# Hybrid attention block on one core: in the first seven attention units a group's fill is written ahead of the products of the group behind it

## The chip, the cores and the metric

The kernel runs on 1 core of a Trainium2 chip. A core has a matrix engine (TensorE, in the profile PE for matmuls and PEld for weight loads), VectorE (DVE), ScalarE (ACT), GpSimd (POOL) and SyncE (SP, which here only starts transfers). The metric is the device time of one execution in microseconds; less is better.

## The reference

A decoder block on x (1024 rows of 1024), all in float32. It normalises x, projects it, and runs two attention branches on the projections: "fox", 8 heads of width 64 with a forgetting bias, and "diff", 4 heads with two query and key pairs each, whose softmaxes are subtracted. Cut to what matters:

```python
h = rms_norm(x, g_pre)
qa, ka, va, fa, za, qb, kb, vb, zb, gates = split(h @ w_in)
ya = merge(fox(qa, ka, va, log_sigmoid(fa + b))) * silu(za)     # softmax(q k^T / 8 + c_t - c_s) v
qd, kd = rope(qb), rope(kb)
yb = merge((softmax(q1 k1^T) - lam * softmax(q2 k2^T)) vb)      # per diff head
yb = rms_norm(yb, g_subln) * (1 - lam_init) * silu(zb)
merged = sigmoid(g_a) * (ya @ w_branch[0]) + sigmoid(g_b) * (yb @ w_branch[1])
out = x + rms_norm(merged @ w_out, g_post)
```

## The kernel before

**Number format.** Every float32 operand of a large matmul is split in a high part (rounded) and a low part (the rest), and a product is three matmuls (high by high, high by low, low by high) or two. So each matrix needs a cast (ACT or POOL) and a subtraction (mostly DVE) before PE can use it.

**Stages.** First x is normalised and transposed to hT and the values are projected (L214, up to about 107 us). Then come eight attention units: units 0 to 3 are the diff heads, units 4 to 7 two fox heads each. Then the gates (L830, x_g), the branch matrices (L990) and the output matrix (L830, x_o) follow.

**One attention unit.** Queries are taken in groups of 256 rows. A diff unit has four groups, g = 0 to 3, in this order; a fox unit has eight, g = 3, 3, 2, 2, 1, 1, 0, 0 (two heads each). A group with index g sees 256(g+1) keys. It has two parts in the text:

- *Rows* (`s_row`, L492 to L501, and `row`): the logits Sd or Sf by two matmuls, a DVE instruction that scales them, adds the bias and finds the extreme (L495), the exponential on ACT, and the scaling of the result. In diff units POOL and ACT scale the two softmaxes (L592, L594) and POOL adds them (L595). The result lies in tiles Pd or Pf, six of them in all.
- *Products* (`products`, `av`): P is transposed in blocks on PE (ptd or ptf, L522; 4g + 3 transposes a group), cast on ACT (L525), the rest subtracted on DVE (L526), and multiplied with V (ypd or ypf, L546). The result is taken out (ACT L602, or ACT L632 and DVE L633) and stored in y_d.

**The fill.** Beside its groups each unit has a list of other work, `fill`: the four chunks that project the next unit's keys and queries (pk and pq, L334, each 24 matmuls of 128x512 on a bank of pool `pj`, which has two), in most units two chunks of a z projection (pz; four in unit 7), and in units 3 to 6 the sums of squares of an earlier diff head (`sum_squares`, ssq, L448 and L449, and a small transfer task). A chunk of a diff unit's key or query is rotated afterwards: ACT copies it (L362), four transfers swap its parts (L366), DVE multiplies (L368), POOL multiplies the swapped part (L369) and DVE adds (L370). Then every key or query chunk is split (L378, L379) and copied to its tiles (L381, L382); a z chunk is copied and stored. The first chunk of each matrix loads its weights (`load_w`, L314 to L324).

**The order in the text.** Each unit's loop goes over its groups. After a group's rows come the products of the group before it (`pend`, across the border of two units too), and then as many fill tasks as bring the done share of the list up to the done share of the unit's weights, 4g + 3 a group. In unit 7 the share is tripled and the loop ends differently (a tail that is written by hand, with gate pieces put after given matmuls).

**The order on the chip.** The kernel is built with `schedule_with_timeline_sim=True`: the framework plans, from the text, in which order each engine gets its instructions, so that matmuls of rows, products and fill come mixed on PE. Tiles, banks and semaphores are set by it as well.

Of the kernel before, what the change touches and what calls it, by code (L numbers as in the profile page):

```python
# [50 lines left out]
def tile_hybrid_block(  # L51
# [288 lines left out]
    with ExitStack() as st:  # L340
# [75 lines left out]
        def z_tasks(t):  # L416
            return spill_tasks(f"z{t}", (ZA + t * P) if t < 4 else (ZB + (t - 4) * P), z_d[t])
# [20 lines left out]
        def sum_squares(t, c):  # L438

            sl = slice(c * CH, (c + 1) * CH)  # L440
            sq = stg.tile([P, CH], F32, tag="raw", name=f"sq{t}_{c}", bufs=4)
            nc.sync.dma_start(sq, y_d[t][:, sl])
            nc.scalar.activation(sq, sq, AF.Square)
            hi, lo = (stg.tile([P, CH], F32R, tag="sw", name=f"sq{part}{t}_{c}") for part in range(2))
            nc.scalar.copy(hi, sq)
            nc.gpsimd.tensor_tensor(lo, sq, hi, op=ALU.subtract)
            ps = pj.tile([P, CH], F32, tag="pj", name=f"ssq{t}_{c}")[0:32]
            nc.tensor.matmul(ps, lhsT=onesr, rhs=hi, start=True, stop=False)  # L448
            nc.tensor.matmul(ps, lhsT=onesr, rhs=lo, start=False, stop=True)  # L449
            nc.scalar.copy(sq[0:1], ps[0:1])  # L450
            nc.sync.dma_start(ss_d[t:t + 1, sl], sq[0:1])

        def subln_scales(t):
            rs = sub_rs[:, t]
            nc.sync.dma_start(rs, ss_d[t].rearrange("(p j) -> p j", j=8))
            rstd_of(rs, rs, P, SUB_EPS)
            nc.sync.dma_start(rs_d[t].rearrange("(p j) -> p j", j=8), rs)
# [96 lines left out]
        def products(trans, prod, g):  # L554
            for jj in range(g + 1 + SKEW):
                if jj <= g:
                    trans(jj)
                if jj >= SKEW:
                    prod(jj - SKEW)
# [91 lines left out]
        def forget_sums():  # L651

            fgf = fg.rearrange("p a b -> p (a b)")
            fs = pp.tile([P, 4, 64], F32, tag="P", name="fs")
            fn, fe, fu, fc = (fs[:, n, :] for n in range(4))
            nc.vector.tensor_scalar(fn, fgf, -1.0, None, op0=ALU.mult)
            nc.vector.tensor_tensor(fn, fn, fgf, op=ALU.min)
            nc.scalar.activation(fe, fn, AF.Exp)
            nc.vector.tensor_scalar(fu, fe, 1.0, None, op0=ALU.add)
            nc.vector.tensor_scalar(fc, fu, -1.0, None, op0=ALU.add)  # L660
            nc.vector.tensor_tensor(fc, fe, fc, op=ALU.subtract)
            nc.scalar.activation(fn, fu, AF.Ln)
            nc.vector.reciprocal(fu, fu)
            nc.vector.tensor_tensor(fc, fc, fu, op=ALU.mult)
            nc.vector.tensor_tensor(fn, fn, fc, op=ALU.add)
            nc.vector.tensor_scalar(fe, fgf, 0.0, None, op0=ALU.min)
            nc.vector.tensor_tensor(fe, fe, fn, op=ALU.subtract)
            lf = pp.tile([8, S], F32, tag="P", name="lf")
            cum = pp.tile([8, S], F32, tag="P", name="cum")
            ones8 = pp.tile([8, S], F32, tag="P", name="ones8")  # L670
            nc.gpsimd.memset(ones8, 1.0)
            for half in range(2):
                tp = tps.tile([P, CH], F32, tag="tp", name=f"ft{half}")
                for q in range(4):
                        b = half * 4 + q
                        nc.tensor.transpose(tp[0:8, q * P:(q + 1) * P], fe[:, b * 8:(b + 1) * 8], ident)
                nc.scalar.copy(lf[:, half * CH:(half + 1) * CH], tp[0:8, :])
            nc.vector.tensor_tensor_scan(cum, ones8, lf, initial=0.0, op0=ALU.mult, op1=ALU.add)
            nc.vector.tensor_scalar(cum, cum, -8.0, None, op0=ALU.mult)
            nc.sync.dma_start(cum_d, cum)  # L680
# [7 lines left out]
        for u in range(8):  # L688
            load, load_v, groups = nxt or unit_attn(u, T)
            nxt = None  # L690
            if u == 0:
                vload.append(load_v)
            if u == 1:
                forget_sums()
            load()
            fill = []
            if u + 1 < 8:
                T, tasks = unit_proj(u + 1)
                fill += tasks
            for t in ZFILL[u]:  # L700
                fill += z_tasks(t)
            for t in SFILL[u]:
                fill += [lambda t=t, c=c: sum_squares(t, c) for c in range(2)]
                fill.append(lambda t=t: subln_scales(t))
            late = [fill.pop(), gate[0]] if u == 7 else []
            total = sum(s[0] for s in groups)
            done, nf = 0, 0
            for n, (wgt, rws, prd) in enumerate(groups):
                if n == len(groups) // 2 and u < 7:
                    nxt = unit_attn(u + 1, T)  # L710
                    vload.append(nxt[1])
                for r in rws:
                    r()
                mark = lasts[0]
                if pend and (u < 7 or n <= TAIL):
                    products(*pend())
                if u == 7 and n >= TAIL:
                    tail.append(prd)
                pend = prd
                done += wgt  # L720
                while nf < len(fill) and nf < len(fill) * done * (3 if u == 7 else 1) / total:
                    fill[nf]()
                    nf += 1
                if u == 7:
                    for f, a, b in LATE[n]:
                        with tc.issue_after(mark):
                            late[f](range(a, b))
                    if n == GFILL:
                        break
# [503 lines left out]
```

## Time and profile before

| | |
|---|---|
| median of 3 runs | 900.85 us (899.52 to 901.63) |
| the profiled execution | 899.54 us, of which 897.8 us from first to last instruction |
| HBM traffic | 139 GB/s over the span |
| PE, mean of one 128x512 matmul of a fill chunk (pq, high part) | 395 ns as recorded; matmuls overlap |
| one transposing matmul (ptd) | 272 ns as recorded, the median |
| cast (phd, ACT) and subtraction (pld, DVE) after it | 567 and 680 ns, medians |
| POOL's sum of two softmaxes (L595) | 454 to 2899 ns, median 1438 |

The profile is of one execution. Busy time of an engine is the time in which at least one of its instructions runs; waits are idle time of an engine just before an instruction, put down to whatever ended last. In a timeline row the first number is the start in us from the first instruction, the second the length of the merged instructions, x the count, and a bracket gives the idle time before it and what ended it.

### The profile page before, as it was taken

What the parts mean: (1) busy time and instruction counts of PE and PEld (TensorE: products, weight loads), DVE (VectorE), ACT (ScalarE), POOL (GpSimd) and SP (SyncE); (2) the same over time, 40 slices, a digit from 0 to 9 for tenths busy, and PEclk for the clock granted to TensorE, in tenths of its full rate; (3) what the DMA queues carried; (4) which work ended last, traced back from release to release, by engine and by line L of the source; (5) the groups of instructions that cost most, each with busy time, mean ns of one, the idle gap of its engine ahead of it and who ended that gap; (6) DMA issues with size and microseconds to landing.
All of it is one profiled execution on the core that took longest, in us unless ns stands there. A gap on an engine that the chain in (4) does not pass through costs nothing.

```text
span 897.8 us, 13825 instructions
## 1 busy us (share of the span) xinstructions
PE 881.9 (98%) x4612; PEld 746.7 (83%) x4612; DVE 580.4 (65%) x1124; ACT 429.0 (48%) x864; POOL 408.9 (46%) x401
## 2 busy tenths in 40 slices
PE   8999999999999999999999999999999999999997
PEld 6999987788888888888888888888888888888885
DVE  6666555767666744456647556626776897648896
ACT  7423224665756654365545646624453362314352
POOL 2234224645646535254344435426534323483963
PEclk9999999999999999999999999999999999999999
DMA  8576656756657763635636430297766599210495
GB/s 306 188 254 245 215 164 158 179 137 170 155 137 184 183 177 77 187 94 133 188 94 155 141 106 30 88 411 240 235 202 213 168 359 312 78 41 1 123 197 172
DMA packets 138186, 154.81 MB, mean 172 GB/s; under 512 B 12145, under 2 KB 98161, under 8 KB 137090
## 3 DMA queue, kind: packets, MB, share of 16 engines
q1 hardware_dynamic: 133744, 151.55, 56.1%
q0 software_dynamic: 4224, 2.10, 2.1%
q8 instruction: 37, 0.61, 0.3%
q14 instruction: 35, 0.29, 0.1%
q10 hardware_dynamic: 146, 0.27, 0.1%
HBM read 86.17 MB, written 38.34 MB: 139 GB/s over the span
## 4 chain that ended last, share of the span: by engine, by line
PE 87%; DMA 3%; DVE 3%; SPq 2%; ACT 2%; POOL 2%; issue 1%; POOLq 0%; DVEq 0%; ACTq 0%
PE x_g L830 15%; PE pv L214 10%; PE pb L990 10%; PE pz L334 9%; PE x_o L830 8%; PE pk L334 7%; PE pq L334 7%; PE ypf L546 3%; PE ptf L522 3%; PE ypd L546 2%; PE Sf L492 2%; PE Sf L493 2%; PE ptd L522 1%; PE Sd L492 1%; PE Sd L493 1%
## 5 line engine op out<-in xcount | busy, mean ns | idle before, releaser
L214 PE MATMUL pv<-wvhi,hT 128*128 128x264 f32 (+2 forms) x384 | 88.6, 325 | 0.0
L334 PE MATMUL pq<-hT,hi_q 128*128 128x512 f32 x256 | 82.1, 395 | 0.0
L334 PE MATMUL pz<-hT,hi_z 128*128 128x512 f32 x256 | 81.6, 394 | 0.4 <-DVE rotq L368 0.3
L334 PE MATMUL pk<-hT,hi_k 128*128 128x512 f32 x256 | 81.7, 393 | 0.0
L990 PE MATMUL pb<-yT,hi_br 128*128 128x512 f32 x256 | 79.0, 389 | 0.0
L830 PE MATMUL x_g<-T,a_g 128*128 128x512 f32 x336 | 78.0, 391 | 0.0
L830 PE MATMUL x_o<-wo_op,a_o 128*128 128x512 f32 x324 | 74.8, 392 | 0.0
L830 PEld LDWEIGHTS x_g<-T,a_g 128*128 128x128 f32 x336 | 63.1, 188 | 13.8
L830 PEld LDWEIGHTS x_o<-wo_op,a_o 128*128 128x128 f32 x324 | 60.7, 188 | 13.9 <-DVE a_o L767 0.5
L214 PEld LDWEIGHTS pv<-wvhi,hT 128*128 128x128 f32 x384 | 64.8, 192 | 5.7
L526 DVE TENSOR_TENSOR plf<-ptf,phf 128x512 fp32r<-128x512 f32 (+1 forms) x80 | 50.1, 635 | 25.1 <-ACT phf L525 24.4
L501 ACT ACTIVATE Pd<-Pd,mxd 128x128 f32<-128x128 f32 (+7 forms) x64 | 49.8, 779 | 33.4 <-DVE mxd L495 33.3
L618 POOL TENSOR_TENSOR cb<-cb,trim 128x128 f32<-128x128 f32 x64 | 29.3, 462 | 74.6 <-DVE mxf L495 51.6
L214 PE MATMUL pv<-wvlo,hT 128*128 128x256 f32 (+2 forms) x192 | 61.7, 326 | 0.0
L501 ACT ACTIVATE Pf<-Pf,mxf 128x1024 f32<-128x1024 f32 (+3 forms) x64 | 49.8, 779 | 24.5 <-DVE mxf L495 22.4
L830 PE MATMUL x_g<-hT,a_g 128*128 128x512 f32 x252 | 59.1, 392 | 0.0
L623 POOL TENSOR_SCALAR Pf<-Pf,lf 128x1024 f32<-128x1024 f32 (+3 forms) x64 | 47.9, 753 | 20.9 <-DVE lf L622 17.6
L525 ACT CAST phf<-ptf 128x512 fp32r<-128x512 f32 (+1 forms) x80 | 42.6, 543 | 30.7 <-PE ptf L522 26.4
L990 PEld LDWEIGHTS pb<-yT,hi_br 128*128 128x128 f32 x256 | 48.0, 188 | 10.4 <-issue 0.4
L830 PEld LDWEIGHTS x_g<-hT,a_g 128*128 128x128 f32 x252 | 47.3, 188 | 10.4
L334 PEld LDWEIGHTS pz<-hT,hi_z 128*128 128x128 f32 x256 | 47.3, 188 | 9.5 <-DVE rotq L368 0.6
L334 PEld LDWEIGHTS pq<-hT,hi_q 128*128 128x128 f32 x256 | 47.2, 188 | 8.9
(277 smaller groups left out, 2289.2 us busy)
## 6 DMA issues: line engine op xcount, KB each, us to landing
t_d<-t SPq DMA_DIRECT2D x16, 512.0 KB, 4.0
T<-t_d SPq DMA_DIRECT2D x8, 1024.0 KB, 11.0
raw<-in_w_in_dram SPq DMA_DIRECT2D x14, 512.0 KB, 5.5
vb_d<-vbs SPq DMA_DIRECT2D x8, 512.0 KB
va_d<-vas SPq DMA_DIRECT2D x8, 512.0 KB, 3.8
raw_k<-in_w_in_dram SPq DMA_DIRECT2D x8, 512.0 KB, 4.4
raw_q<-in_w_in_dram SPq DMA_DIRECT2D x8, 512.0 KB, 4.7
V<-vb_d SPq DMA_DIRECT2D x4, 1024.0 KB, 6.2
```

The source lines that it names most:

```text
L214: nc.tensor.matmul(ps[n], lhsT=hT[hp][k // 4][i // 4][:, k % 4, hs], rhs=wt[k][:, a:b], start=first, stop=(k == KT - 1 and hp == 1))
L334: mm = nc.tensor.matmul(ps, lhsT=a[:, k, :], rhs=hT[h][k // 4][c][:, k % 4, :], start=(k == 0 and a is hi and h == 0), stop=(k == KT - 1 a ...
L492: nc.tensor.matmul(ps, lhsT=A[:, qs], rhs=B[:, a:b], start=True, stop=False)
L501: nc.scalar.activation(pr[:, 0:n], pr[:, 0:n], AF.Exp, bias=mx[:, len(pcs) - 1:len(pcs)], scale=-1.0, accum_out=le)
L522: lasts[0] = nc.tensor.transpose(pt[:, o * P:(o + 1) * P], rows[2 * g + r][:, j * P:(j + 1) * P], ident).ins
L525: nc.scalar.copy(ph[:, 0:n], pt[:, 0:n])
L526: nc.vector.tensor_tensor(pl[:, 0:n], pt[:, 0:n], ph[:, 0:n], op=ALU.subtract)
L546: lasts[0] = nc.tensor.matmul(o, lhsT=a, rhs=b[:, src], start=(j == 0 and n == 0), stop=(odd == 1 and jj == g and n == len(prods) - 1)).ins
L618: nc.gpsimd.tensor_tensor(diag, diag, trim, op=ALU.add)
L623: held[0] = nc.gpsimd.tensor_scalar(p1[:, 0:n], p1[:, 0:n], l1, 1.0, op0=ALU.mult, op1=ALU.mult).ins
L830: nc.tensor.matmul(x[m], lhsT=a[:, ai, k, :], rhs=right[m][bi][k], start=(k == 0 and n == 0), stop=(k == 3 and n == 2))
L990: nc.tensor.matmul(ps, lhsT=a[:, kk, :], rhs=yT[g][h][:, k % 2, sl], start=(k == 0 and a is hi and h == 0), stop=(k == 3 and a is lo))
```

## The change

In units 0 to 6 a group's fill share moves from behind the products of the group before it to ahead of them. The share is as large as before; unit 7 keeps its order. No instruction is added or removed, no tile changes its size or its number of buffers.

```diff
                 for r in rws:
                     r()
                 mark = lasts[0]
+                done += wgt
+
+                def more(nf):
+                    while nf < len(fill) and nf < len(fill) * done * (3 if u == 7 else 1) / total:
+                        fill[nf]()
+                        nf += 1
+                    return nf
+
+                if u < 7:
+                    nf = more(nf)
                 if pend and (u < 7 or n <= TAIL):
                     products(*pend())
                 if u == 7 and n >= TAIL:
                     tail.append(prd)
                 pend = prd
-                done += wgt
-                while nf < len(fill) and nf < len(fill) * done * (3 if u == 7 else 1) / total:
-                    fill[nf]()
-                    nf += 1
+                nf = more(nf)
                 if u == 7:
                     for f, a, b in LATE[n]:
                         with tc.issue_after(mark):
```

So for group n, with R for rows, P for products and F for a fill share, the text read R(n), P(n-1), F(n), R(n+1), P(n), F(n+1); it now reads R(n), F(n), P(n-1), R(n+1), F(n+1), P(n).

## The prediction

> **What bounds the kernel now.** First the page, for the engine that has no room; then the busy time by stage; then the waits of that engine; last its timeline, for the order of its work.
>
> ```profile
> span 897.8 us, 13825 instructions
> PE 881.9 (98%) x4612; PEld 746.7 (83%) x4612; DVE 580.4 (65%) x1124; ACT 429.0 (48%) x864; POOL 408.9 (46%) x401
> PEclk9999999999999999999999999999999999999999
> PE 87%; DMA 3%; DVE 3%; SPq 2%; ACT 2%; POOL 2%; issue 1%; POOLq 0%; DVEq 0%; ACTq 0%
> ```
>
> TensorE (PE) is busy 881.9 of 897.8 us, at full granted clock in every slice, and holds 87% of the chain that ended last. VectorE (DVE), the next compute engine, is at 65%. So only idle time of PE can be won. Where it lies, from the busy time of each engine in three stretches (the attention units run from about 107 to 592 us; I put the borders at 154 and 530 us for reasons given below):
>
> ```profile
> core 0: us, PE busy (x) PEld busy (x) DVE busy (x) ACT busy (x) POOL busy (x), PEclk, DMA share, GB/s
> 107.00:154.00 47.00, 45.75 (x210) 37.36 (x209) 25.70 (x52) 16.24 (x37) 13.81 (x14) 1.00 0.57 158
> 154.00:530.00 376.00, 372.52 (x2082) 319.40 (x2080) 227.40 (x580) 209.53 (x443) 185.06 (x201) 1.00 0.57 148
> 530.00:592.00 62.00, 60.68 (x369) 52.39 (x369) 38.27 (x111) 39.05 (x85) 29.65 (x41) 1.00 0.31 112
> ```
>
> In the long middle stretch PE idles 376.00 - 372.52 = 3.48 us. The waits of PE in it, with who ended them (total, times, longest):
>
> ```profile
> PE ptd L522 <- POOL Pd L595: 0.9, 1, 0.9
> PE Sd L492 <- DVE mxd L495: 0.6, 2, 0.4
> PE ssq L448 <- ACT sq L445: 0.5, 1, 0.5
> PE pz L334 <- DVE rotq L368: 0.3, 1, 0.3
> PE ypf L546 <- DVE ys L633: 0.3, 1, 0.3
> PE ypf L546 <- DVE plf L526: 0.2, 1, 0.2
> PE ptf L522 <- DVE plf L526: 0.2, 1, 0.2
> ```
>
> They sum to 3.0 us. The products wait 0.9 + 0.3 + 0.2 + 0.2 = 1.6 us of it (transposes ptd, ptf and matmuls ypf), the fill 0.5 + 0.3 = 0.8 us (ssq, pz), the logits 0.6 us (Sd). No wait is as long as 1 us. A wait costs more than its idle time. A 128x512 matmul is recorded with 0.39 us but followed by the next after 0.23 (24 of them in 5.49 us, below), so the first 0.16 us of a delay don't show as idle; and the pair that starts after the wait at 171.11 (below) takes 0.72 where others take 0.62. That makes 0.26 us more at each of the eight waits, an estimate of 2.1 us in all.
>
> **What the planned order already does.** The text of the kernel isn't the order on PE: a matmul chain written in one piece is broken up on the chip by whatever else was ready in the framework's planning. What stands earlier in the text goes first when both are ready. So it matters where the fill already runs ahead of the products. Unit 1, PE's timeline:
>
> ```profile
> 187.55 0.62 PE L334 MATMUL pq<-hT,hi_q 128*128 128x512 f32 x2
> ...
> 194.35 0.39 PE L334 MATMUL pq<-hT,lo_q 128*128 128x512 f32 x1
> 194.58 0.40 PE L334 MATMUL pk<-hT,hi_k 128*128 128x512 f32 x1
> 194.82 1.03 PE L522 MATMUL ptd<-ident,Pd 128*128 128x128 f32 x8
> ```
>
> The pq chunk is the fill share of unit 1's second group; the eight transposes at 194.82 are the first of unit 0's last group. In the text those products stand ahead of this whole chunk, and of the one before it, but their rows were not ready, so two chunks of fill went first. The swap changes nothing there. The other kind of place, unit 0:
>
> ```profile
> 153.69 0.61 PE L334 MATMUL pq<-hT,hi_q 128*128 128x512 f32 x2
> 154.15 0.27 PE L522 MATMUL ptd<-ident,Pd 128*128 128x128 f32 x1
> 154.17 0.48 PE L334 MATMUL pq<-hT,lo_q 128*128 128x512 f32 x1
> ...
> 158.20 0.40 PE L334 MATMUL pq<-hT,lo_q 128*128 128x512 f32 x1
> 159.50 0.76 PE L522 MATMUL ptd<-ident,Pd 128*128 128x128 f32 x5 [0.90 <-POOL Pd L595]
> ```
>
> Here a transpose of the second group breaks into the fill share of the third: products were ready first, and the swap turns the two round. Following chunks and products by name through the whole timeline, I count 30 fill shares with products pending behind them in units 0 to 6; in 17 of them the products start before the share's last matmul. 154.15 is the first of the 17; none lies in unit 6, whose products start after the projections of their share. In unit 7, from 530 us on, the text stays as it was. So the first and last stretch should keep their idle time, but for what is handed on from the middle.
>
> **The change part by part.** It adds and removes no instruction: PE's 2082 matmuls of the middle stretch stay, each of the same shape. What moves is a share, one to three chunks. A chunk costs PE this, in the chain of work that ended last (start, us, what):
>
> ```profile
> 107.55 5.49 PE pk L334 x24
> ```
>
> So 5.49 us a chunk, and products that were ready may be put off by 5.5 to 16 us at the 17 places, the fill brought forward by the length of the products that it overtakes. Work that only changes places on a busy engine costs nothing: 0 us, as long as something ready stands next on PE. Changing between transposes and other matmuls could have had a price; the row that follows the eight transposes of 194.82 bounds it:
>
> ```profile
> 195.61 0.47 PE L334 MATMUL pk<-hT,hi_k 128*128 128x512 f32 x1
> ```
>
> It takes 0.47 against 0.39 us in the rows above, so under 0.1 us a change, and as many changes go as come. I take 0.
>
> What each wait of PE becomes. (a) 159.50, 0.9 us: the fill of that share was done at 158.60 and the next chunk (pz) began at 161.12 in the same timeline, so nothing was ready. With the fill first the same work is done by then in another order, and the wait stays: 0. (b) The logits' 0.6 us: they stand ahead of both in the text, as before: 0. (c) The products' other 0.7 us (ys, plf, three waits, with 3 x 0.26 us 1.5): these follow a transpose or an evacuation that the plan took as just in time. Products that go later stand behind a reserve: between 0 and -1.5, I take the middle, -0.7. (d) ssq 0.5: its chunk now stands ahead of the products, which must cover the same chain of load, square and cast; between -0.5 and +0.5, I take 0. (e) pz 0.3: it waits for a bank that the rotation of an earlier chunk must leave. This kind grows, because fill that is placed as soon as the plan thinks it ready has no reserve: between 0 and the second rival's price; I take one more such wait, 0.28 + 0.26 = +0.5.
>
> The share's other engines move too. Its transfers on SP's queue (weights, half swaps, stacked copies) go ahead of the products' stores of y_d, which nobody reads for a whole unit or more:
>
> ```profile
> 160.57 0.54 SPq L603 DMA_DIRECT2D y_d<-ys  x1
> 161.16 0.46 SPq L382 DMA_DIRECT2D TB<-loq  x1
> 161.71 2.46 SPq L366 DMA_DIRECT2D swk<-rawk  x4
> ```
>
> The loads of X that the next group needs stand behind both in the text: 0. On POOL the products have nothing. On DVE they do; its longest kind of wait in a rotation, over the whole run, and one rotation with the PE row that waited for it:
>
> ```profile
> DVE rotq L370 <- POOL swq L369: 15.1, 7, 5.2
> ```
>
> ```profile
> 170.36 0.69 DVE L368 TENSOR_TENSOR rotq<-pq,cosT 128x512 f32<-128x512 f32 x1 [0.34 <-ACT rawq L362]
> ...
> 171.11 0.72 PE L334 MATMUL pz<-hT,hi_z 128*128 128x512 f32 x2 [0.28 <-DVE rotq L368]
> ```
>
> The sum of a rotation (rotq L370) waits for POOL, 15.1 us in 7 times, and what DVE has next waits with it. Products' subtractions that used to go ahead of it may now queue behind it, and PE's products behind them. Unseen in this trace; between 0 and the 2.2 us of one such wait. I take 0, since rows nearest to it (the two 0.2 us waits for plf) say that PE feels little of DVE.
>
> Sum of (a) to (e) and the queues: 0 + 0 - 0.7 + 0 + 0.5 + 0 = -0.2 us. The profiled execution took 899.54 us, 1.7 us more than its span; the median of the runs is 900.85 (899.52 to 901.63). -0.2 us from the median gives **900.6 us**. What a measurement can tell from no change here is about 0.2%, 1.8 us.
>
> [...]
>
> **The rivals.** *Faster: the reserve pays.* Products placed behind a share of fill no longer meet rows or casts that are late on the chip, also at (a), because the plan itself comes out otherwise. For it: 1.6 of the 3.0 us are waits of products. Against it: half of them has nothing else to run. Price: the 3.48 us of idle time and the 2.1 us hidden beside it are all there is; the products' part, 1.6 us and four times 0.26, gives -2.6: 898.2 us. *Slower: the fill becomes what is late.* At 170.36 the rotation left its bank 11.8 us after its chunk's last matmul (158.6), more than the 5.49 us that a following chunk fills. Written first, a share takes its second chunk up as soon as the plan sees the bank free, and a chip that is a little later than the plan stops PE at its head, with the products behind it. The place is the start of a chunk in the 17 turned shares; its price is 0.54 us each, 0.28 of 171.11 and 0.26 beside it. With every second of them hit, 9 x 0.54 = 4.9 us, 905.7 us; it decides from 4 on (2.2 us). Against it: units 3 to 6 fill mostly with chunks that need no rotation. *It does nothing:* the plan turns little round even at the 17 places; 900.85 us, inside the forecast's case.
>
> **How the numbers follow.** Forecast, within 0.2%: 0.38, since 13 of 30 shares keep their order and in the others work only trades places on a full engine. Faster: 0.32. Slower: 0.30; the ceiling of a gain is low, but nothing bounds a loss as tightly. Range: down to all idle time of the middle stretch gone with half of what hides beside it (900.85 - 3.5 - 1.1 = 896.2), up to the second rival's 905.7 and the 0.8 us by which the slowest run shown lies over the median: 906.5.
>
> **What would show it.** The two traces should agree up to about 154 us, where the pq chunk should now run through without the transpose. PE's matmul count should stay; PE's idle time in the middle stretch should stay between 2 and 5 us, with fewer waits of ptf and ypf and more of pk, pq or pz for rotation or POOL. I am wrong if PE idles over 6 us there (the fill is late, or DVE holds the products), under 1.5 us (the reserve was worth more), or if the last units, whose text hardly changes, differ much: then the order planned at the end hangs on what comes before.

## The result, and the profile after

The changed kernel takes 911.34 us (median of 6 runs, 908.4 to 919.27), the kernel before 900.5 us (6 runs, 899.03 to 901.63). The ratio is 1.0129, with a 95% interval from 1.0088 to 1.0169. The forecast was no change, 900.6 us, and its range ended at 906.5 us; the time lies outside it. The profiled execution took 909.24 us.

The page of the changed kernel, first the busy times, then the engines' shares of the chain that ended last:

```profile
span 907.5 us, 13827 instructions
PE 884.3 (97%) x4612; PEld 748.2 (82%) x4612; DVE 575.7 (63%) x1124; ACT 428.9 (47%) x864; POOL 409.1 (45%) x401
PE 73%; DMA 8%; POOL 5%; DVE 5%; issue 3%; ACT 3%; SPq 2%; POOLq 0%; DVEq 0%; ACTq 0%
```

The count of matmuls is the same. PE was busy only 2.4 us longer, the span grew by 9.7 us, and PE's share of the last chain fell from 87% to 73%: PE waits for others now. Where, from the busy time of each engine by stretch (columns as before: stretch, its length, busy time and instructions of PE, PEld, DVE, ACT, POOL, granted clock, DMA):

```profile
154.00:200.00 46.00, 42.60 (x218) 35.31 (x217) 31.30 (x73) 26.97 (x52) 25.91 (x20) 0.96 0.59 146
200.00:262.00 62.00, 61.78 (x343) 52.96 (x343) 38.29 (x102) 36.99 (x83) 33.17 (x29) 1.00 0.56 139
262.00:330.00 68.00, 67.05 (x362) 56.93 (x360) 39.48 (x102) 38.09 (x81) 36.01 (x32) 1.00 0.71 184
330.00:430.00 100.00, 97.60 (x549) 84.31 (x550) 52.64 (x135) 49.07 (x102) 42.74 (x52) 1.00 0.50 131
430.00:530.00 100.00, 96.64 (x559) 83.56 (x558) 57.61 (x160) 53.40 (x117) 43.81 (x62) 1.00 0.49 133
530.00:592.00 62.00, 60.69 (x383) 52.66 (x382) 41.99 (x123) 39.88 (x91) 28.50 (x45) 1.00 0.22 68
```

Length less PE's busy time gives its idle time. From 154 to 530 us it is 3.40 + 0.22 + 0.95 + 2.40 + 3.36 = 10.33 us where it was 3.48, 6.85 us more. In the last stretch it is 1.31 where it was 1.32. The 0.96 in the first row is a second loss: 3.4 us at half clock, 1.7 us (last section). The two make 8.55 of the 9.7 us. Most of the rest stands ahead of the change: the attention units begin at 108.31 instead of 107.38 us.

What ended PE's waits from 154 to 530 us (us in total, times, longest):

```profile
PE ssq L448 <- ACT sq L445: 2.3, 2, 1.2
PE ptd L522 <- POOL Pd L595: 2.1, 2, 1.4
PE pk L334 <- ACT sz L433: 1.2, 2, 1.0
PE Sf L492 <- DVE mxf L495: 1.2, 1, 1.2
PE ptf L522 <- DVE plf L526: 1.1, 1, 1.1
PE ypf L546 <- DVE plf L526: 0.8, 1, 0.8
PE ypd L546 <- DVE pld L526: 0.8, 2, 0.5
PE ypd L546 <- ACT phd L525: 0.4, 1, 0.4
PE Sd L492 <- DVE mxd L495: 0.3, 1, 0.3
```

Before, there were eight waits, none as long as 1 us. Now there are thirteen and six of them last 1 us or more. They don't have one releaser: the products wait for the parts of P (plf, pld, phd: 3.1 us), for POOL's sum of two softmaxes (2.1), the sums of squares for ACT (2.3), the fill for a bank (1.2), the logits for DVE (1.5). By engine that is 4.2 us for DVE, 3.9 for ACT and 2.1 for POOL. The view says what the next matmul in PE's planned order waited for; whether something further back in that order was ready, it doesn't say.

The first long one that is new lies at the border of units 0 and 1. PE's timeline, rows with a wait in brackets:

```profile
180.05 0.39 PE L334 MATMUL pz<-hT,lo_z 128*128 128x512 f32 x1
...
182.33 0.50 PE L546 MATMUL ypd<-phd,V 128*128 128x256 f32 x2 [0.38 <-ACT phd L525]
183.06 0.39 PE L546 MATMUL ypd<-pld,V 128*128 128x256 f32 x1 [0.23 <-DVE pld L526]
...
185.38 0.73 PE L334 MATMUL pk<-hT,hi_k 128*128 128x512 f32 x2 [1.01 <-ACT sz L433]
```

and ACT's timeline in the same microseconds:

```profile
183.30 1.28 ACT L662 ACT_TABLE_LOAD   x1
...
184.76 1.06 ACT L433 COPY sz<-pz 128x512 f32<-128x512 f32 x2
```

The last matmul of the last z chunk starts at 180.05. From there PE has logits and one group of products, which waits for ACT (0.38 us) and for DVE (0.23). The next fill (pk) needs a bank, and ACT copies the finished z chunks out only at 184.76, behind casts and a table load. In the kernel before, transposes of these products (175.30 to 176.56) stood between the matmuls of the z chunks, the last of which starts at 178.52, and ACT copied the z chunks out ahead of the table load:

```profile
181.35 1.06 ACT L433 COPY sz<-pz 128x512 f32<-128x512 f32 x2
...
183.93 1.28 ACT L662 ACT_TABLE_LOAD   x1
```

### The profile page after: what moved, and what is told of

Its sections match the earlier page's. It is cut to its first block, busy times and chain, and to the rows that moved or that the text cites. A ratio compares the mean times of both kernels' runs of the same rounds, so it can differ in the third digit from the quotient of the medians.

```text
span 907.5 us, 13827 instructions
## 1 busy us (share of the span) xinstructions
PE 884.3 (97%) x4612; PEld 748.2 (82%) x4612; DVE 575.7 (63%) x1124; ACT 428.9 (47%) x864; POOL 409.1 (45%) x401
## 4 chain that ended last, share of the span: by engine, by line
PE 73%; DMA 8%; POOL 5%; DVE 5%; issue 3%; ACT 3%; SPq 2%; POOLq 0%; DVEq 0%; ACTq 0%
PE x_g L837 15%; PE pb L997 10%; PE pv L214 9%; PE x_o L837 8%; PE pz L334 7%; PE pk L334 5%; PE pq L334 5%; PE ypf L546 3%; PE ptf L522 2%; DMA cb<-cum_d 2%; POOL Pd L595 2%; SPq L366 2%; DMA swk<-rawk 1%; PE Sf L492 1%; DMA swq<-rawq 1%
## 5 line engine op out<-in xcount | busy, mean ns | idle before, releaser
L334 PEld LDWEIGHTS pk<-hT,hi_k 128*128 128x128 f32 x256 | 47.3, 188 | 10.1 <-ACT sz L433 1.7
L592 POOL TENSOR_SCALAR Pd<-Pd,l,nlam 128x128 f32<-128x128 f32 (+7 forms) x32 | 31.5, 984 | 52.7 <-DVE l L591 48.7
```

What stands on the lines that cost most here:

```text
L334: mm = nc.tensor.matmul(ps, lhsT=a[:, k, :], rhs=hT[h][k // 4][c][:, k % 4, :], start=(k == 0 and a is hi and h == 0), stop=(k == KT - 1 a ...
L592: nc.gpsimd.tensor_scalar(p2[:, 0:n], p2[:, 0:n], l2, nlam, op0=ALU.mult, op1=ALU.mult)
```

## The experiments

Theory: the fill is cover. As the lowest-priority work it was there whenever a step of the products was late; ahead of them it is used up first. Rivals: the fill itself is what is late (its banks, its sums of squares); any other text gives a worse plan; one border or one engine carries it all. Ratios are to the kernel before on the same chip, with 95% intervals.

**Which units.** The condition `if u < 7:` ahead of the share was narrowed to the diff units, to the fox units, and to all but unit 0:

```diff
-                if u < 7:
+                if u < 4:          # e1_diff
+                if 4 <= u < 7:     # e2_fox
+                if 0 < u < 7:      # e7_not_u0
```

> Fill ahead of products in units 0 to 3 only. Theory A (each turned share costs where it stands): in the changed kernel about 4.8 us more PE idle time lies in units 0 to 3 and about as much in units 4 to 6, so +5 us (905 to 906) here, and the waits of PE up to 332 us as in the changed kernel, those behind as before. Theory B (any new text order makes the framework plan anew, and the plan before happens to fit the chip): nothing adds up; anything from 0 to +11, and waits that neither kernel has.

> Fill ahead of products in units 4 to 6 only. Theory A: the rest of the loss, about +5 us (905 to 906), with the two waits of ssq and the two of plf that the changed kernel has, and no low clock at 163 us. Theory B: no relation to the first run; the sum of the two need not be the loss of both.

> Fill ahead of products in units 1 to 6; unit 0 keeps the order of before. In the changed kernel and in the run with units 0 to 3, 154 to 200 us hold 3.1 us more PE idle time than before and granted-clock loss of about 1.8 us. Theory U (unit 0's shares make this: its last products are put off into the forget sums at the border of units 0 and 1): those 5 us go, 905 to 907, no low clock there. Theory S (the loss is the same kind at every border and share): only unit 0's share of it, a seventh, goes: 909 to 911.

Measured: 909.0 us, 1.0103 (1.0082 to 1.0123) with the diff units; 903.56 us, 1.0038 (1.0026 to 1.005) with the fox units; 907.45 us, 1.0087 (1.0066 to 1.0109) without unit 0. The two parts add up to the whole within the intervals (1.03 + 0.38 against 1.29%), which fits separate losses, though not the equal halves that theory A expected. What unit 0 has of it can't be told: the intervals with and without it overlap, and in e7 the idle time only moves. It goes from 154 to 200 us (table below), but from 262 to 330 us there is a new wait of 3.02 us, of the sums of squares for ACT.

**Which part of the share.** Sums of squares left behind the products; only key and query chunks ahead; only shares that hold no key or query chunk ahead (z chunks and sums of squares):

```diff
+                def more(nf, end):
+                    while nf < end and nf < len(fill) * done * (3 if u == 7 else 1) / total:
...
+                    nf = more(nf, len(fill) - 3 * len(SFILL[u]))   # e3_ss_back
+                    nf = more(nf, len(tasks))                      # e14_qk_ahead
...
+                nf = more(nf, len(fill))
```

```diff
-                if u < 7:
+                if u < 7 and nf >= len(tasks):                     # e15_z_ahead
```

> As the changed kernel, but the sums of squares stay behind the products; only projections go ahead. If the sums of squares are the fill that is late (ssq waits 2.3 us here, 0.5 before), the waits of ssq go back to about 0.5 and the time falls by 2 to 3 us, to 908 to 909. If the products' casts are what is late (plf, pld, phd, together 3.3 us in the changed kernel, 0.9 before), no change: 911. Theory B: anything from 900 to 911.

> Units 0 to 6, only key and query chunks ahead of the products; z chunks and sums of squares stay behind. If the z chunks are what is missed as cover at the end of a unit (they are the last shares of units 0 and 1 and need no rotation, so they can run at any time), most of the loss goes: 900 to 904. If the next unit's keys and queries written early are what costs, it stays: 908 to 912.

> The complement: only z chunks and sums of squares ahead of the products, and only in shares that have no key or query chunk. If the z chunks are the missed cover: 906 to 912, with the waits at 182 to 186 and at 237 us. If keys and queries are what costs: 899 to 903.

Measured: 912.21 us, 1.0137 (1.0117 to 1.0158) with the sums of squares behind, so their place isn't the cause though PE waits 2.3 us for them (2.4 us in e3). 902.98 us, 1.0046 (1.0031 to 1.0061) with key and query chunks ahead. 910.91 us, 1.013 (1.0097 to 1.0163) with z chunks and sums of squares ahead: they alone give as much as the whole change. By e3 the sums of squares have no part in it that shows, so I put it down to the z chunks; no run moves z chunks without any sum of squares through all units. A z chunk needs no rotation and no copies for the next unit; its result is only stored, so it could stand anywhere. The losses don't add (1.30 and 0.46 against 1.29%).

PE's idle time by stretch, worked out as above from the same view of each kernel, shows where; the last column is the time at a granted clock of 0.50 in the attention units (last section), of which half is lost where PE is busy:

| us | 154-200 | 200-262 | 262-330 | 330-430 | 430-530 | sum | half clock |
|---|---|---|---|---|---|---|---|
| before | 1.54 | 0 | 0.60 | 1.04 | 0.30 | 3.48 | 0 |
| after | 3.40 | 0.22 | 0.95 | 2.40 | 3.36 | 10.33 | 3.4 |
| e1_diff | 4.65 | 0.18 | 1.58 | 2.10 | 1.47 | 9.98 | 6.8 |
| e2_fox | 1.32 | 0 | 0.81 | 0.85 | 3.95 | 6.93 | 0 |
| e7_not_u0 | 1.28 | 0.65 | 4.53 | 0.85 | 3.54 | 10.85 | 6.8 |
| e14_qk_ahead | 1.66 | 0.78 | 0.80 | 0.61 | 1.06 | 4.91 | 3.4 |
| e15_z_ahead | 3.75 | 3.92 | 0 | 1.07 | 3.47 | 12.21 | 0 |
| e12_last | 3.71 | 3.32 | 0 | 1.22 | 0.28 | 8.53 | 0 |
| e13_notlast | 1.73 | 0.39 | 3.41 | 1.13 | 1.36 | 8.02 | 10.2 |

So key and query chunks ahead (e14) cost PE 1.43 us of idle time and about 1.7 us of half clock; z chunks (e15) cost 8.73 us of idle time and no half clock.

In this table two places come back whenever z chunks go ahead there: the stretch with the border of units 0 and 1 (3.4 to 4.7 us where it was 1.5) and units 5 and 6 (3.4 to 4.0 where it was 0.3). In the first, 1.43 of the changed kernel's 3.40 us are the wait for POOL at 160.67, ahead of the border. Three kernels below have z chunks ahead in units 5 and 6 and idle less there: e6 (1.51), e17 (0.50) and e18 (0.52). Between the two places a third moves about with the plan. One of its forms, e15's unit 1, on DVE and on PE:

```profile
235.53 2.31 DVE L370 TENSOR_TENSOR rotq<-rotq,swq 128x512 f32<-128x512 f32 x1 [3.30 <-POOL swq L369]
237.76 0.68 DVE L495 CUSTOM_DVE_ANT_0 Pd<-Sd,dmask 128x512 f32<-128x512 f32 x1
```

```profile
237.01 0.39 PE L334 MATMUL pz<-hT,lo_z 128*128 128x512 f32 x1
238.50 0.50 PE L492 MATMUL Sd<-KB,TB 128*128 128x512 f32 x1 [1.11 <-DVE mxd L495]
```

DVE stands 3.30 us for the rotation's swapped part and then adds for 2.31 (0.69 is the median of this sum in the changed kernel; last section); the logits behind it in DVE's order come out at 237.76, and their bank is free late. The last z matmul starts at 237.01, and then PE waits 1.11 us.

The kernel before has the same jam on DVE once, 1.81 us and 2.32 us with logits behind it, and PE's fill in the same microseconds:

```profile
271.32 2.32 DVE L370 TENSOR_TENSOR rotk<-rotk,swk 128x512 f32<-128x512 f32 x1 [1.81 <-POOL swk L369]
273.56 0.68 DVE L495 CUSTOM_DVE_ANT_0 Pd<-Sd,dmask 128x512 f32<-128x512 f32 x1
```

```profile
271.36 0.48 PE L334 MATMUL pq<-hT,hi_q 128*128 128x512 f32 x1
...
275.11 0.39 PE L334 MATMUL pk<-hT,lo_k 128*128 128x512 f32 x1
```

There PE runs fill from 271.36 to 275.34, when the next logits follow, and doesn't wait at all. This pair is the most direct sign of cover on record: a late DVE costs PE time where the fill has run out, and none where it hasn't. The two jams aren't the same length, so it is a sign and not a proof.

**Which share of a unit.** In the diff units only the last share ahead, or all but the last; and in all seven units only the first half of each share's step:

```diff
-                if u < 7:
+                if u < 4 and n == 3:     # e12_last
+                if u < 4 and n < 3:      # e13_notlast
```

```diff
+                half = done + wgt / 2    # e10_half
                 done += wgt
...
+                def more(nf, done=done):
...
+                    nf = more(nf, half)
```

> Fill ahead of products only for the last group's share in units 0 to 3; in units 0 to 3 together the full swap cost 9 us (1.0%). Theory B3 (the loss sits at the borders of units, where the last products meet the next unit's first rows and nothing else): 904 to 908, with the waits at 182 to 186, 237 and 330 to 333 us of the full swap. Theory S (each share costs alike): a quarter of the loss, 901 to 903.

> Units 0 to 3, fill ahead of products for the first three groups' shares only: the rest of the swap that cost 1.03% in these units, of which the last group's shares alone cost 0.85%. Theory B3 (the loss sits at the borders of units): 0.1 to 0.3%, 900 to 902. Theory P (every move of the fill costs some 4 us, whichever and whichever way, since half of it, the other direction and SKEW 2 all cost 0.4 to 0.5%): 0.4% or more, 903 to 905, and the parts don't add up.

> As the changed kernel, but of a share only the part up to half of the group's weight goes ahead of the products (of two chunks the first), the rest stays behind them. Theory R (the fill that stands behind the products is PE's cover for their late rows and casts; with all of it ahead, nothing ready is left): most of the loss goes, 901 to 905. Theory O (a chunk ahead of products costs by itself, by putting rows' and products' work behind it on ACT and DVE): at least half of the loss stays, 906 to 911.

Measured: 906.81 us, 1.0085 (1.0067 to 1.0102) for the last share alone, 904.89 us, 1.0068 (1.0043 to 1.0093) for the others, 903.2 us, 1.0047 (1.0031 to 1.0063) for half. The last share, which in units 0 and 1 is their two z chunks and nothing else, costs at least as much as the other three together by the medians (the intervals overlap). But the two parts sum to 1.53% where both at once cost 1.03% (e1): each edit gives another plan, and a sum over parts isn't exact here.

**Whether any new plan costs.** The kernel before with queries ahead of keys in the fill list, with the forget sums (a block of small work on ACT and DVE) one unit later, and with each share one group later:

```diff
-            tasks = [mk("k", 0, kc + t * P), mk("q", 0, qc + t * P),
-                     mk("k", 1, kc + t * P), mk("q", 1, qc + t * P)]
+            tasks = [mk("q", 0, qc + t * P), mk("k", 0, kc + t * P),     # e4_qk
+                     mk("q", 1, qc + t * P), mk("k", 1, kc + t * P)]
```

```diff
-            if u == 1:
+            if u == 2:                   # e9_fs2_before
                 forget_sums()
```

```diff
-                done += wgt
+                last_n = n == len(groups) - 1                # e5_lag
+                if u == 7 or last_n:
+                    done += wgt
                 while nf < len(fill) and nf < len(fill) * done * (3 if u == 7 else 1) / total:
...
+                if u < 7 and not last_n:
+                    done += wgt
```

> The kernel before, but in each unit the query chunk is written ahead of the key chunk instead of behind it; fill and products keep their order. It has no reason to cost anything: same work, same dependencies. Theory A: within 0.3% of before (898 to 903). Theory B (every new plan fits worse than this one): slower by 3 us or more, with new waits of PE spread over the units.

> Control for the run before it: the kernel before with the forget sums at the start of unit 2. Both theories: within 0.3% (898 to 903). If it gains 3 us or more, the forget sums cost the kernel before too, and a gain of the run before it is no evidence on the swap.

> The kernel before with the fill moved the other way: each group's share is written one group later, and the last group of a unit takes what is left. Theory R: PE keeps more cover within a unit but has a long run of fill at its end, with the products of the last groups behind: 899 to 904 . Theory O: fewer chunks ahead of products, so no loss or a gain, 897 to 901. If any shift of the fill costs, 905 or more.

Measured: 899.06 us, 0.9994 (0.9981 to 1.0007); 900.7 us, 1.0012 (1.0001 to 1.0024); 903.7 us, 1.005 (1.0031 to 1.0069). None of these new plans costs anything like 1.29%. Fill that comes later isn't better either: the kernel before lies between two worse orders. A rival stays open here, the one that e13's expectation names: that every move of the fill costs some 4 us, whichever way. Five moves that differ (e2, e10, e14, e5 and e13) cost 0.38 to 0.68%. It can't explain the 1.3% of the z chunks, but up to half of that may be of its kind.

**The border, and the reserve of the products.** The changed kernel with the forget sums out of the border of units 0 and 1; SKEW, the number of blocks by which a product's transposes run ahead of its multiplications, at 2 instead of 1, in the changed kernel and in the one before:

```diff
-            if u == 1:
+            if u == 2:                   # e8_fs2, on the changed kernel
                 forget_sums()
```

```diff
-SKEW = 1
+SKEW = 2                                 # e6_skew on the changed kernel, e11_skew_before on the one before
```

> The changed kernel with the forget sums (with their two table loads of 1.28 us on ACT) written at the start of unit 2 instead of unit 1. Theory U: the waits at 182 to 186 us (products for casts, the key chunk for the z copy queued behind a table load) go: 3 to 5 us less, 906 to 908, unless they come back at the border of units 1 and 2. Theory S: no change, 910 to 912.

> The changed kernel with products written with two transposed blocks ahead of the multiplication instead of one (SKEW 2). Theory B2 (once the fill is done ahead, nothing lies between a block's transposes, cast and subtraction and its product, so PE waits for pld, plf, phd: 3.3 us in the changed kernel, 0.9 before): these waits shrink below 1 us and the time falls by 2 to 4 us, 907 to 909. If the products are late for their rows or for a busy ACT and DVE, no gain: 910 to 913.

> Control for SKEW 2 in the changed kernel (0.8% over before instead of 1.3%): the kernel before with SKEW 2. If the reserve of a second block helps products that have lost their cover, nothing here: 898 to 902. If it helps any order by the same 4 us, 895 to 897.

Measured: 909.22 us, 1.0105 (1.0089 to 1.0121); 905.84 us, 1.0081 (1.0049 to 1.0113); 902.56 us, 1.0043 (1.0027 to 1.006). Moving the block that collides at the border wins little, if anything (the intervals overlap), so the collision with the table load is one form of the wait and not its cause. SKEW 2 costs the kernel before 0.43%, more than either expectation allowed, and the changed kernel lies lower with it (1.29 to 0.81%). The intervals overlap, and the waits for plf, pld and phd are still 2.2 us from 154 to 530 us (3.1 without it, under 1 expected). So it isn't shown that an earlier transpose stands in for the lost cover.

**Which engine is late.** In e2 (fox units alone) most of PE's long waits from 330 to 530 us are for DVE (3.5 us; 1.3 us are of the sums of squares for ACT). The stretch in which the z chunk runs, and the next, in e2:

```profile
488.50:496.50 8.00, 8.00 (x45) 6.92 (x44) 3.33 (x12) 3.90 (x8) 4.17 (x6) 1.00 0.61 188
496.50:504.00 7.50, 6.26 (x44) 5.52 (x43) 7.22 (x20) 6.85 (x14) 5.15 (x6) 1.00 0.57 174
```

and the same pair in the kernel before:

```profile
490.00:498.60 8.60, 8.60 (x50) 7.50 (x49) 4.16 (x11) 3.90 (x9) 2.99 (x6) 1.00 0.67 219
498.60:504.00 5.40, 5.32 (x39) 4.65 (x39) 4.84 (x12) 4.23 (x8) 1.77 (x3) 1.00 0.59 173
```

Fill needs little of DVE: 3.33 of 8.00 us in e2, 4.16 of 8.60 before. Behind it rows, products and a weight come at once: in e2 DVE is busy 7.22 of 7.50 us and PE idles 1.24. Before, DVE was nearly as full in its second stretch (4.84 of 5.40), for a shorter time, and PE idled 0.08. Over the 20 us from 484 to 504 DVE does no more in e2 (13.58 us against 14.20); only its place is another. The row, and what DVE did ahead of it:

```profile
502.67 0.45 PE L492 MATMUL Sf<-KB,TB 128*128 128x384 f32 x1 [1.24 <-DVE mxf L495]
```

```profile
500.61 1.33 DVE L324 TENSOR_TENSOR lo_z<-raw_z,hi_z 128x1024 fp32r<-128x1024 f32 x1
...
501.94 0.67 DVE L495 CUSTOM_DVE_ANT_0 Pf<-Sf,cb 128x512 f32<-128x512 f32 x1
```

A weight's subtraction of 1.33 us stands ahead of the scaling (501.94) that frees the bank. So the subtractions of nine fill weights of units 4 to 6 were moved to POOL, in the kernel before (e16) and in e2 (e17), and then all of units 0 to 6 in the changed kernel (e18; they are 20, seven of keys, seven of queries and six of z, where the expectation says 21):

```diff
-                        box[kind] = load_w(f"{kind}{u}", w_cols(c0))
+                        box[kind] = load_w(f"{kind}{u}", w_cols(c0), lo_pool=u >= 5)     # e18: u >= 1
...
-                        box[0] = load_w(nm, w_cols(c0))
+                        box[0] = load_w(nm, w_cols(c0), lo_pool=nm in ("z3", "z4", "z5"))    # e18: z0 to z5
```

> The kernel before, with the subtraction that gives a fill weight its low part moved from VectorE to GpSimd for the fill of units 4 to 6 (nine loads, 1.22 us of VectorE each). It is the base for the next run. PE idles only 1.3 us from 330 to 530 us in the kernel before, so neither theory gives it a gain: 1.000, within 0.2%, unless GpSimd's own products of rows come later for it.

> The change in units 4 to 6 alone (1.0038 against before), with the same nine subtractions on GpSimd. Theory, VectorE bunches: with the fill as one run VectorE has little to do beside it (3.33 of 8.00 us) and then rows, products and a weight's subtraction come at once (7.22 of 7.50 us), and PE waits 1.24 us for a logits bank and 1.2 us for a product's subtraction. Then taking nine times 1.22 us from VectorE must shorten these waits, and the ratio to the run before falls to 1.002 or less. Rival, the order alone: the planner puts too little beside the products whatever VectorE has to do; the ratio to the run before stays between 1.003 and 1.005.

> The full change with the subtraction of every fill weight of units 0 to 6 on GpSimd (21 loads, 1.22 us of VectorE each). Theory, VectorE bunches in units 0 to 3 as it did in units 4 to 6, where nine such moves took the ratio from 1.0038 to 0.9987: it falls from 1.0129 to 1.005 or less, and PE idles under 6 us from 154 to 530 us. Rival: in units 0 to 3 another engine is what is late (ScalarE's casts and z copies at 180 to 186 us, GpSimd's sum of two softmaxes before the transposes at 159 us, and this sum comes later still behind a subtraction of 2.4 us): only the part of units 4 to 6 comes back, and the ratio stays at 1.008 or above.

Measured: e16 899.38 us, 1.0007 (0.9998 to 1.0016); e17 897.95 us, 0.9987 (0.9975 to 1.0000); e18 908.89 us, 1.0098 (1.0078 to 1.0117). With nine subtractions off DVE the order of e2 costs nothing any more: 897.95 / 899.38 = 0.9984 against e16. From 330 to 530 us e17 has one kind of wait left,

```profile
PE Sf L492 <- DVE mxf L495: 0.9, 2, 0.7
```

and in the stretch that stood above DVE is busy 5.79 of 7.50 us:

```profile
496.50:504.00 7.50, 7.01 (x48) 6.01 (x46) 5.79 (x14) 5.58 (x12) 2.95 (x4) 1.00 0.45 123
```

A reservation: the plan differs as well. The two subtractions that stood directly ahead of e2's waits were of unit 7's weights, which e17 leaves on DVE but places elsewhere, and e2's wait of the sums of squares for ACT is gone too. A new plan alone moved other kernels by up to 0.5% (e5). What is shown is that the loss of the fox units went away together with DVE's load; that this load made it is the likely reading, not that one subtraction did.

In units 0 to 3 the same remedy doesn't help. e18's waits from 154 to 530 us:

```profile
PE Sd L492 <- DVE mxd L495: 4.8, 6, 1.7
PE pz L334 <- DVE rotk L368: 2.9, 1, 2.9
...
PE Sf L492 <- DVE mxf L495: 0.3, 1, 0.3
```

Only 0.3 us is left of the fox units' waits (Sf); PE idles 0.52 us from 330 to 530 us instead of 5.76. But it idles 5.85 + 2.42 + 1.67 = 9.94 us from 154 to 330 us (4.57 in the changed kernel). The longest wait shows why. PE, DVE and POOL around it in e18:

```profile
160.84 1.19 PE L334 MATMUL pz<-hT,hi_z 128*128 128x512 f32 x2 [2.88 <-DVE rotk L368]
```

```profile
155.86 2.86 DVE L370 TENSOR_TENSOR rotq<-rotq,swq 128x512 f32<-128x512 f32 x1 [3.77 <-POOL swq L369]
159.40 0.69 DVE L379 TENSOR_TENSOR loq<-rotq,hiq 128x512 fp32r<-128x512 f32 x1 [0.68 <-ACT hiq L378]
160.01 0.68 DVE L368 TENSOR_TENSOR rotk<-pk,cosT 128x512 f32<-128x512 f32 x1
```

```profile
155.78 2.39 POOL L324 TENSOR_TENSOR lo_z<-raw_z,hi_z 128x1024 fp32r<-128x1024 f32 x1
```

The z chunk waits for the bank that the rotation of a k chunk leaves (160.01). That stands on DVE behind the sum of a q chunk's rotation, which waits 3.77 us for POOL and then takes 2.86 us beside POOL's moved subtraction (0.69 us elsewhere; last section). So the weights' subtractions on DVE don't carry the loss of the diff units: with DVE relieved of them, POOL, the rotations and the logits behind them are late.

e17 is the fastest version that was run, but it can't be told from the kernel before: its interval touches 1 and its gain is inside the 0.2%.

## Why the prediction was wrong

- *What stays as it was*: right. No transpose breaks into the pq chunk of 153.69 us any more (its last matmul starts at 158.63, the transposes at 158.86; logits and multiplications of other products still stand between its matmuls), the matmuls are the same in number, and unit 7 idles as before (1.31 us).
- *"Work that only changes places on a busy engine costs nothing: 0 us, as long as something ready stands next on PE"*: this step failed, by its own condition. I counted 17 shares that trade places and asked only what stands there during the trade. What counts is what stands at the end: PE has then logits and products in a row, whose rows, casts and subtractions come one behind another. That z chunks, on which nothing waits, give as much as the whole change (e15) speaks for it, and so do half a share (e10), with which most of the loss is gone, and the jam at 271 us in the kernel before; no run isolates it. Nor did the count say where: none of the 17 lies in unit 6, and two of the six long waits do (1.05 us at 487.61 and 1.23 at 508.39, ahead of and behind its z chunks). Instead of 0 us the change cost 6.85 us of idle time from 154 to 530 us and 1.7 us of half clock.
- *Wait (a), 0.9 us, "stays"*: it became 1.43 us, at 160.67. *(c), the products' casts, -0.7*: the sign was wrong. plf, pld, phd and ys made 0.7 us and make 3.1 (plf, pld and phd; ys is gone). I took "behind a share" as a reserve; the products are later, but what they need from DVE is later too: in e2 DVE is busy 3.33 of 8.00 us beside the fill and 7.22 of 7.50 behind it. *(d), the sums of squares, 0*: 0.5 became 2.3 us, but leaving them behind (e3) won nothing, so this wait is where PE stops and not why. *(b), the logits' 0.6, "0"*: 1.5 us, with DVE as their releaser.
- *DVE, "between 0 and the 2.2 us of one such wait. I take 0"*: too low. The rotation's sum is the form that e15 shows (2.31 us on DVE, 1.11 on PE); and the weights' subtractions of 1.2 us, which belong to a moved share too, weren't in the sum. In the fox units the loss went away with DVE's load (e17).
- *Slower: the fill becomes what is late* had the sign, not the mechanism. Fill that waits for its bank makes 1.2 us (pk), where the rival asked 4.9 us for 905.7; the fill's other wait, the sums of squares for ACT (2.3 us), isn't for a bank. So 9.0 of the 10.2 us in the list of waits have other releasers.
- *What would make it wrong*, "PE idles over 6 us there (the fill is late, or DVE holds the products)": both, in part. Of the 10.2 us in the list of waits DVE ends 4.2, and the fill's own waits (pk and ssq) are 3.5.
- *Missing from the sum*: the granted clock. "No wait is as long as 1 us" was true of the kernel before; the change made longer ones, and one of them cost 1.7 us more in half clock.

What stays open: why half a share, shares one group later, and key and query chunks ahead each cost 0.5%, with 4.9 to 8.2 us of PE's idle time (and 3.4 us at half clock in the last of them); how much of the full loss is of this kind; and which engine is late first in units 0 to 3.

## What to carry to other kernels

Work with slack that is planned at the lowest priority can be the cover of everything else; before it is moved ahead of a chain, ask what is left for the busy engine when the chain's next link is late, not only whether the engine is busy during the move. Separating work that loads one side engine from work that doesn't can bunch that engine, even if its share over the whole run is 65%. A cheap test is to move only the part that nobody waits for: here this part alone, the z chunks, cost as much as the whole change.

## What the runs showed of the hardware

I had not expected a wait of 1 to 3 us to slow PE beyond its end. In the changed kernel, PE's wait and the stretches behind it:

```profile
160.67 0.77 PE L522 MATMUL ptd<-ident,Pd 128*128 128x128 f32 x5 [1.43 <-POOL Pd L595]
```

```profile
154.00:162.70 8.70, 6.91 (x38) 5.49 (x37) 5.83 (x12) 2.94 (x7) 5.96 (x6) 1.00 0.70 176
162.70:166.10 3.40, 3.40 (x10) 2.62 (x9) 3.02 (x8) 3.17 (x6) 2.12 (x3) 0.50 0.87 214
```

From 162.7 us, 2 us after the wait's end, the granted clock is 0.50 for 3.4 us. In these microseconds a 128x512 matmul follows the one before it after 0.43 us (four starts from 164.25 to 165.53), where ahead of the wait and from 166.28 on it follows after 0.23. So 1.7 us of work are lost by the clock, 1.6 by that spacing, more than by the wait itself. e9_fs2_before shows it after a wait of 2.28 us that ends at 160.71, and e8_fs2 that a wait of 1.74 us can pass without it:

```profile
160.90:164.30 3.40, 3.40 (x12) 2.66 (x12) 3.02 (x12) 1.35 (x3) 1.50 (x2) 0.50 1.11 274
```

```profile
158.90 0.77 PE L522 MATMUL ptd<-ident,Pd 128*128 128x128 f32 x5 [1.74 <-POOL Pd L595]
```

```profile
159.00:163.00 4.00, 3.64 (x19) 2.80 (x20) 3.62 (x10) 1.87 (x4) 1.95 (x2) 1.00 1.05 251
```

In the attention units of the profiled executions of this study, no run whose waits all stay under 1 us shows half clock (before, e10, e16, e17: 1.00 in every stretch from 154 to 530 us); behind waits of 1 to 2 us it came sometimes (in e14, whose longest is 1.30 us, and not in e2, whose longest is 1.31), and with the six over 2 us (2.03 to 3.28) always. The length of the one wait doesn't decide it: behind a wait of 1.15 us for plf it came in e8 (0.51 from 487.3 to 490.7 us) and not in e2 (1.00 from 482 to 488.5 us). In e8 another wait, of 0.64 us, had ended 1.9 us before this one did; in e2 it was one of 0.24. With the two of 3.02 and 3.28 us (e7, e13) the clock was 0.50 for 6.8 us, twice 3.4 (328.5 to 335.3 and 328.9 to 335.7 us), and this began while PE still waited (to 329.80 and 331.02). What decides it, these rows don't show.

The clock also orders the changed kernel's runs: 908.4 us at a mean granted clock of 0.999, 909.24 at 0.996, 911.19 to 912.33 at 0.994 and 0.995, 919.27 at 0.990. The profiled execution lost 1.7 us to it; the slower ones, by their clocks, lost more.

The second surprise is how DVE and POOL hold each other up. The sum of a rotation (L370) adds two tiles. Its 0.69 us became 2.86 us beside POOL's subtraction in e18 (155.78 to 158.17, above), 0.55 us after whose end it ended; and 2.31 us in e15, again 0.54 us after the end of POOL's instruction:

```profile
235.46 1.84 POOL L595 TENSOR_TENSOR Pd<-Pd,Pd 128x768 f32<-128x768 f32 x1
```

With 0.55 and 0.54 us of it left behind POOL's end, it got little of its 0.69 us done until POOL was done. POOL's instruction started first both times, by 0.08 and 0.07 us. In one place where DVE's started first, POOL's took longer: in e18 DVE's subtraction at 159.40 (above) takes its 0.69 us, and POOL's sum, which starts 0.04 us behind it, 1.78 us:

```profile
159.44 1.78 POOL L595 TENSOR_TENSOR Pd<-Pd,Pd 128x512 f32<-128x512 f32 x1
```

In the changed kernel the same two stand the other way round, with 0.04 us between their starts; POOL's sum takes 1.26 us and DVE's subtraction 1.77:

```profile
159.35 1.26 POOL L595 TENSOR_TENSOR Pd<-Pd,Pd 128x512 f32<-128x512 f32 x1
```

```profile
159.39 1.77 DVE L379 TENSOR_TENSOR loq<-rotq,hiq 128x512 fp32r<-128x512 f32 x1 [0.69 <-ACT hiq L378]
```

Not every instruction of POOL does it, though. In the changed kernel DVE's sum takes its 0.69 us beside POOL's scaling by two factors, which started 0.05 us ahead of it:

```profile
158.01 0.69 DVE L370 TENSOR_TENSOR rotq<-rotq,swq 128x512 f32<-128x512 f32 x1 [1.68 <-POOL swq L369]
```

```profile
157.96 1.30 POOL L592 TENSOR_SCALAR Pd<-Pd,l,nlam 128x512 f32<-128x512 f32 x1
```

So work moved from DVE to POOL can come back as DVE's time: the weight's subtraction that e18 took off DVE here is 1.23 us long on DVE in the changed kernel (155.11), and the rotation's sum beside it on POOL became 2.17 us longer (2.86 against 0.69).
